# Stick-breaking attention scores: the low parts of two query tiles against the keys' high parts on the two row halves of TensorE, and projection units spread over all attention steps

## The chip, the cores and the metric

The kernel runs on one core of one Trainium2 chip. The metric is the device time of one execution in microseconds (us). A core has five engines: TensorE (PE; its weight loads are listed apart as PEld), VectorE (DVE), ScalarE (ACT), GpSimd (POOL) and SyncE (SP). Each works through its own queue in order; they wait for one another by semaphores. ACT and SP also issue the DMA transfers (ACTq, SPq in the rows).

## The reference

One layer of a hybrid mixer over 2048 tokens of width 1024: a modulated RMS norm, one wide projection, three kinds of mixing side by side (four heads of gated linear attention, GLA; four of HGRN, computed in the same chunked way; four of stick-breaking attention), a gated output projection and a last norm. The part that the change touches is the stick-breaking attention, with four heads of 64:

```python
def stick_breaking_attn(q, k, v):
    ...
    for i in range(t // SB_BLOCK):
        ...
        z = jnp.einsum('bhtd,bhsd->bhts', q_blk, k_blk).astype(jnp.float32) * scale
        ...
        log_beta = jax.nn.log_sigmoid(z)
        log_1m_beta = jnp.where(strict, jax.nn.log_sigmoid(-z), 0.0)
        between = lax.cumsum(log_1m_beta, axis=3, reverse=True) - log_1m_beta
        weights = jnp.where(strict, jnp.exp(log_beta + between), 0.0)
        outs.append(jnp.einsum('bhts,bhsv->bhtv', weights.astype(v.dtype), v_blk))
```

Everything is fp32 in the reference.

## The kernel before

The kernel runs in stages: modulation, norm and the first projections (to about 340 us), value columns and forget gates, the attention stage (402 to 870 us), the recurrent stage of GLA and HGRN (to about 1080 us), and the output projection.

**Split numbers.** A projection is done in a faster number format of TensorE (`F32R`), with each fp32 operand split into a high and a low part and three products: high by high, high by low and low by high. A *unit* (`fm_unit`, lines 149 to 157) is one such projection of 128 columns over 512 tokens: 24 matmuls of 128x512 (L154, L155, L156).

**Attention.** `sb_stream` (L680 on) yields 80 steps. Its loops run over the four heads, over the eight pairs `ip` of query tiles of 128 tokens (u = 0, 1 in a pair), and over the blocks `J` of 512 keys from the diagonal down. The query's tile `Q` holds the high part in `Q[:, 0]` and the low part in `Q[:, 1]`, each twice: on rows 0 to 63 and again on rows 64 to 127. The keys' tile `K[J]` holds the high part on rows 0 to 63 and the low part on rows 64 to 127. So L725 forms high times high plus high times low, and L726 adds low times high plus low times low, each with all 128 rows. A step does, for each u: two score matmuls into a PSUM tile `zt` (three buffers, `psZ`), a sigmoid on ACT (L728, tile `f`), on the diagonal a mask on POOL (L730), a running product on DVE along the keys (L734), up to four transpositions on PE (L738, tile `pt`), and a copy to `PT` on ACT for u = 0 (L741) or DVE for u = 1 (L743). Then come the products with the values (L750, tile `av`), whose 64 columns of output go to the lower half of the partitions for u = 0 and the upper half for u = 1. In the 32 steps whose block holds the diagonal a query tile has 1 to 4 of the 128-key sub-blocks, in the other 48 all four.

**Order.** In this stage a scheduler in the compiler sets the order on each engine from the order in which the program records the work. `interleave` (L760 on) records one step of `sb_stream` or one of 34 units of `fm_stream` (L668 on: the GLA and HGRN features and the gates), five units ahead of the first step and then in the proportion `na` to `nb`. Before, `na` is 80 // 2 = 40, so the units are used up when about half of the 80 steps are recorded. A unit is also held back until the last `av` matmul of two steps earlier has been issued (`SB_LAG`, `marks`). Further gate projections (L260) fill the recurrent stage that follows.

**Elsewhere.** In the output stage `normalise` spreads the eight norm factors over the partitions with L1157, a matmul with 40 rows, 128 columns of weights and 512 streamed columns, which stands among the full matmuls L1192 to L1194; L1137 and L1138 sum squares with 8 columns of weights. In the recurrent stage L917 forms small scores on row halves and column strips, L847 the state updates `U`.

Of the kernel before, what the change touches and what calls it, by code (L numbers as in the profile page):

```python
# [8 lines left out]
F32 = mybir.dt.float32  # L9
F32R = mybir.dt.float32r  # L10
# [8 lines left out]
P = 128  # L19
# [11 lines left out]
SB_LAG = 2  # L31
# [11 lines left out]
def hybrid_mixer_kernel(ctx, tc, x, c, w_ada, b_ada, w_in, w2, bg, gnw, lbl, hnw,  # L43
                        w_out, fnw, masks, sel2, out):
    nc = tc.nc
    mm = nc.tensor.matmul
# [4 lines left out]
    def dram(name, shape, dt=F32):  # L51
        return dp.tile(shape, dt, name=name)
# [6 lines left out]
    s_kc = [dram(f"s_kc{j}", [2, P, T]) for j in range(2)]  # L59
# [75 lines left out]
    def split_w(col0, pool, ncols, step, bufs=None, low=nc.vector):  # L135
        hi = pool.tile([P, KT, ncols], F32R, tag="whi", name="whi", bufs=bufs)
        lo = pool.tile([P, KT, ncols], F32R, tag="wlo", name="wlo", bufs=bufs)
        for s in range(0, ncols, step):
            raw = wp.tile([P, KT, step], F32, tag="wraw", name="wraw")
            nc.sync.dma_start(raw, w_in_v[:, :, col0 + s:col0 + s + step])  # L140
            nc.scalar.copy(hi[:, :, s:s + step], raw)
            low.tensor_tensor(lo[:, :, s:s + step], raw, hi[:, :, s:s + step].bitcast(F32),
                              op=ALU.subtract)
        return hi, lo
# [139 lines left out]
    with tc.manual_schedule(engines={ENG.PE, ENG.DVE, ENG.Activation, ENG.Pool}):  # L284
# [170 lines left out]
        for i in (1, 2):  # L455
            n = ORDER[i]
# [8 lines left out]
    n = ORDER[3]  # L465
# [173 lines left out]
    st2 = ExitStack()  # L639
    kp = st2.enter_context(tc.tile_pool(name="kp", bufs=5, reuse_waits="tile"))  # L640
# [27 lines left out]
    def fm_stream(blocks, after):  # L668
        for col0, chunks, evac in blocks:
            w = split_w(col0, wp, P, P)  # L670
            for n in chunks:
                mark = after()
                if mark is None:
                    fm_unit(w, n, evac)
                else:
                    with tc.issue_after(mark):
                        fm_unit(w, n, evac)
                yield

    def sb_stream(st):  # L680
        sp = st.enter_context(tc.tile_pool(name="sp", bufs=4, reuse_waits="tile"))
        vp = st.enter_context(tc.tile_pool(name="vp", bufs=5, reuse_waits="tile"))
        psZ = st.enter_context(tc.tile_pool(name="psZ", bufs=3, space=PSUM))
        psT = st.enter_context(tc.tile_pool(name="psT", bufs=2, space=PSUM))
        psO = st.enter_context(tc.tile_pool(name="psO", bufs=1, space=PSUM))
        NT = T // P
        for h in range(4):
            j, r0 = h // 2, (h % 2) * 64
            cs = slice(h * 64, (h + 1) * 64)
            vb, vp_ = (s_vc[e:T + e, cs].rearrange("(b p) d -> p b d", p=P) for e in (1, 0))  # L690
            V, Dd = [None] * 4, [None] * 4
            for J in reversed(range(4)):
                Js = slice(4 * J, 4 * J + 4)
                V[J] = vp.tile([P, 4, 64], F32, tag="V", name="V")
                Dd[J] = vp.tile([P, 4, 64], F32, tag="Dd", name="Dd")
                nc.sync.dma_start(V[J], vb[:, Js, :])
                nc.sync.dma_start(Dd[J], vp_[:, Js, :])
                nc.vector.scalar_tensor_tensor(Dd[J], V[J], nm, Dd[J], op0=ALU.mult, op1=ALU.add)
                nc.vector.scalar_tensor_tensor(V[J], V[J], nl, Dd[J], op0=ALU.mult, op1=ALU.add)
            K = [None] * 4  # L700
            for J in reversed(range(4)):
                K[J] = kp.tile([P, 512], F32R, tag="K", name="K")
                for r in range(2):
                    nc.sync.dma_start(K[J][r * 64:(r + 1) * 64].bitcast(F32),
                                      s_kc[j][r, r0:r0 + 64, J * 512:(J + 1) * 512])
            for ip in reversed(range(NT // 2)):
                Q = kp.tile([P, 2, 256], F32R, tag="Q", name="Q", bufs=2)
                for r in range(2):
                    nc.sync.dma_start(
                        Q[r * 64:(r + 1) * 64].bitcast(F32),  # L710
                        s_qc[j][:, r0:r0 + 64, ip * 256:(ip + 1) * 256].rearrange("l p t -> p l t"))
                av = psO.tile([P, P], F32, tag="av", name="av")
                carry = [1.0, 1.0]
                Jtop = (2 * ip) // 4
                for J in reversed(range(Jtop + 1)):
                    top = J == Jtop
                    PTs = []
                    for u in range(2):
                        i = 2 * ip + u
                        nb = (i % 4) + 1 if top else 4  # L720
                        n = nb * P
                        N = max(n, 256)
                        zt = psZ.tile([P, 512], F32, tag="zt", name="zt")
                        us = slice(u * P, (u + 1) * P)
                        mm(zt[:, 0:N], Q[:, 0, us], K[J][:, 0:N], start=True, stop=False)  # L725
                        mm(zt[:, 0:N], Q[:, 1, us], K[J][:, 0:N], start=False, stop=True)  # L726
                        f = sp.tile([P, 512], F32, tag="f", name="f")
                        nc.scalar.activation(f[:, 0:n], zt[:, 0:n], AF.Sigmoid, scale=-0.125)  # L728
                        if top:
                            nc.gpsimd.affine_select(f[:, n - P:n], f[:, n - P:n], pattern=[[-1, P]],  # L730
                                                    base=0, channel_multiplier=1,
                                                    compare_op=ALU.is_gt, fill=1.0)
                        fr = f[:, 0:n][:, ::-1]
                        nc.vector.tensor_tensor_scan(fr, fr, fr, carry[u], op0=ALU.mult, op1=ALU.bypass)  # L734
                        carry[u] = f[:, 0:1]
                        pt = psT.tile([P, 4, P], F32, tag="pt", name="pt")
                        for b in range(nb):
                            nc.tensor.transpose(pt[:, b, :], f[:, b * P:(b + 1) * P], ident)  # L738
                        PT = sp.tile([P, 4, P], F32, tag="PT", name="PT")
                        if u == 0:  # L740
                            nc.scalar.copy(PT[:, 0:nb, :], pt[:, 0:nb, :])  # L741
                        else:
                            nc.vector.tensor_copy(PT[:, 0:nb, :], pt[:, 0:nb, :])  # L743
                        PTs.append((nb, PT))

                    for b in reversed(range(4)):
                        for u, (nb, PT) in enumerate(PTs):
                            if b < nb:
                                diag = top and b == nb - 1
                                last[0] = mm(av[u * 64:(u + 1) * 64, :], (Dd if diag else V)[J][:, b, :],  # L750
                                             PT[:, b, :], start=diag, stop=(J == 0 and b == 0))
                    yield
                ost = sp.tile([P, P], F32, tag="ost", name="ost", bufs=2)
                nc.scalar.copy(ost, av)
                for u in range(2):
                    i = 2 * ip + u
                    nc.scalar.dma_start(s_o[6 + j][r0:r0 + 64, i * P:(i + 1) * P],
                                      ost[u * 64:(u + 1) * 64, :])

    def interleave(a, na, b, nb, first, marks, lead=0):  # L760
        ia = ib = 0
        da = db = False
        for _ in range(lead):
            next(b, None)
            ib += 1
        while not (da and db):
            if not da and (db or ia * nb <= ib * na):
                with tc.issue_after(first):
                    da = next(a, a) is a
                marks.append(last[0].ins)  # L770
                ia += 1
            elif not db:
                try:
                    next(b)
                except StopIteration:
                    db = True
                ib += 1
# [6 lines left out]
    def ev_silu(dst):  # L784
        def f(ps, n):
            sg = stg.tile([P, 512], F32, tag="st", name="sg")
            with tc.issue_after(sig.ins):
# [6 lines left out]
    feat_blocks = []  # L794
# [3 lines left out]
    feat_blocks += [(C_QB + j * P, ORDER, ev_silu(s_feat["qb"][j])) for j in range(2)]  # L798
    feat_blocks += [(gate_cols[j], ORDER[2:], ev_silu(s_gate[j])) for j in range(8)]
    marks = []  # L800
    interleave(sb_stream(st2), 80 // 2, fm_stream(feat_blocks, lambda: marks[-SB_LAG] if len(marks) >= SB_LAG else None),
               34, sig.ins, marks, 5)
    st2.close()
    hpools[ORDER[3]].close()
# [513 lines left out]
```

## Time and profile before

| | |
|---|---|
| median of 3 runs | 1297.59 us (1294.85 to 1298.18) |
| profiled execution, its own time | 1294.26 us |
| its span, first to last instruction | 1292.2 us |
| mean granted TensorE clock | 0.976 |
| PE busy | 1212.9 us (94%) |
| DVE busy | 742.1 us (57%) |
| ACT busy | 471.7 us (37%) |
| POOL busy | 162.9 us (13%) |
| attention stage, first score matmul to last `av` matmul | 402.3 to 869.8 us |

Busy time of PE counts each matmul from its start to its modelled end, and neighbours overlap; the distance from one start to the next is what a matmul costs when PE is full. Idle time of an engine that does not bound a stage costs nothing. The rows that matter stand in a section of their own below.

### The profile page before, as it was taken

To read this page: it belongs to the slowest core of one execution; us is meant where nothing else is said; L and a number is where in the kernel's file an instruction comes from. 1 tells how busy PE (TensorE), PEld (TensorE's weight loads), DVE (VectorE), ACT (ScalarE), POOL (GpSimd) and SP (SyncE) were. 2 spreads that over 40 slices of the span, in tenths; PEclk is the share of its full clock that TensorE was granted. 3 is DMA by queue.
4 is the path that set the end of the run, shared out by engine and by line. 5 is a ranking of instruction groups with operands and counts; after the bars stand their busy time and mean duration, and the time that the engine had idled before them with its cause. 6 is when DMAs were issued, how large, how long until landed. Compare 5 with 4: busy or idle time off the path is not lost.

```text
span 1292.2 us, 22081 instructions
## 1 busy us (share of the span) xinstructions
PE 1212.9 (94%) x8682; PEld 991.8 (77%) x8682; DVE 742.1 (57%) x1268; ACT 471.7 (37%) x860; POOL 162.9 (13%) x197
## 2 busy tenths in 40 slices
PE   7899999999999789999999999998978897999997
PEld 7777789899998667777777776766867774777775
DVE  4866325700009873535545488877776768765652
ACT  3376423421115342322333244543333434253621
POOL 3210000000003300000000001012432312010000
PEclk8999999999999989999999999998988997999999
DMA  9765442422133341322323323127877657464621
GB/s 265 240 232 180 147 126 91 143 82 86 46 99 112 126 106 54 92 72 86 100 68 86 109 73 92 34 62 238 264 222 208 195 174 241 133 224 132 203 82 51
DMA packets 177566, 173.73 MB, mean 134 GB/s; under 512 B 39625, under 2 KB 131882, under 8 KB 177454
## 3 DMA queue, kind: packets, MB, share of 16 engines
q1 hardware_dynamic: 144970, 128.70, 33.7%
q10 hardware_dynamic: 32484, 43.54, 9.7%
q8 instruction: 70, 1.15, 0.4%
q14 instruction: 42, 0.34, 0.1%
HBM read 113.47 MB, written 58.73 MB: 133 GB/s over the span
## 4 chain that ended last, share of the span: by engine, by line
PE 62%; DVE 13%; DMA 6%; issue 5%; ACT 2%; POOL 1%; SPq 0%; ACTq 0%; POOLq 0%; DVEq 0%
PE av L750 6%; PE acc L154 5%; PE acc L156 5%; PE acc L155 5%; PE acc L166 4%; PE acc L168 4%; PE acc L167 4%; PE pt L738 4%; PE acc L260 4%; PE y L1194 4%; PE y L1192 4%; PE y L1193 4%; DMA kt<-s_kb 2%; DVE W L858 2%; DVE f L734 2%
## 5 line engine op out<-in xcount | busy, mean ns | idle before, releaser
L734 DVE TENSOR_TENSOR_SCAN f<-f 128x512 f32<-128x512 f32 (+3 forms) x160 | 169.9, 1091 | 22.0 <-ACT f L728 11.9
L154 PE MATMUL acc<-hTh,whi 128*128 128x512 f32 x400 | 160.1, 402 | 9.9 <-ACT st L185 4.3
L156 PE MATMUL acc<-hTh,wlo 128*128 128x512 f32 x400 | 157.5, 394 | 0.0
L155 PE MATMUL acc<-hTl,whi 128*128 128x512 f32 x400 | 157.4, 394 | 0.0
L166 PE MATMUL acc<-whi,hTh 128*128 128x256 f32 (+1 forms) x512 | 146.2, 285 | 1.5 <-ACT stt L193 1.5
L168 PE MATMUL acc<-whi,hTl 128*128 128x256 f32 (+1 forms) x512 | 145.8, 285 | 0.0
L167 PE MATMUL acc<-wlo,hTh 128*128 128x256 f32 (+1 forms) x512 | 145.6, 284 | 0.0
L260 PE MATMUL acc<-hTh,whi 128*128 128x512 f32 x240 | 103.8, 432 | 1.7 <-ACT hTh L244 1.7
L260 PE MATMUL acc<-hTl,whi 128*128 128x512 f32 x240 | 97.9, 408 | 4.3 <-DVE hTl L250 4.3
L1192 PE MATMUL y<-wh,hTh 128*128 128x512 f32 x256 | 101.8, 398 | 0.0
L1193 PE MATMUL y<-wl,hTh 128*128 128x512 f32 x256 | 101.6, 397 | 0.0
L728 ACT ACTIVATE f<-zt 128x512 f32<-128x512 f32 (+3 forms) x160 | 82.1, 537 | 52.9 <-DVE f L734 24.7
L1194 PE MATMUL y<-wh,hTl 128*128 128x512 f32 x256 | 100.1, 395 | 0.4 <-DVE hTl L1160 0.4
L166 PEld LDWEIGHTS acc<-whi,hTh 128*128 128x128 f32 x512 | 97.8, 191 | 1.9 <-ACT stt L193 1.7
L154 PEld LDWEIGHTS acc<-hTh,whi 128*128 128x128 f32 x400 | 75.5, 189 | 29.9 <-ACT st L185 5.6
L167 PEld LDWEIGHTS acc<-wlo,hTh 128*128 128x128 f32 x512 | 97.8, 191 | 0.1
L168 PEld LDWEIGHTS acc<-whi,hTl 128*128 128x128 f32 x512 | 97.8, 191 | 0.1
L260 PE MATMUL acc<-hTh,wlo 128*128 128x512 f32 x240 | 97.4, 406 | 0.0
L750 PE MATMUL av<-PT,V 128*64 128x128 f32 x960 | 89.7, 282 | 0.6 <-DVE PT L743 0.6
L156 PEld LDWEIGHTS acc<-hTh,wlo 128*128 128x128 f32 x400 | 75.3, 188 | 17.0 <-issue 1.4
L738 PE MATMUL pt<-ident,f 128*128 128x128 f32 x544 | 87.0, 283 | 0.9 <-DVE f L734 0.7
L155 PEld LDWEIGHTS acc<-hTl,whi 128*128 128x128 f32 x400 | 75.6, 189 | 15.2 <-issue 1.0
(206 smaller groups left out, 2106.8 us busy)
## 6 DMA issues: line engine op xcount, KB each, us to landing
wraw<-in_w_in_dram SPq DMA_DIRECT2D x36, 512.0 KB, 4.9
xt<-in_x_dram SPq DMA_DIRECT2D x16, 512.0 KB, 5.2
wa<-in_w_ada_dram SPq DMA_DIRECT2D x16, 512.0 KB, 5.6
Q<-s_qc SPq DMA_DIRECT2D x64, 128.0 KB, 3.1
ot<-s_o SPq DMA_DIRECT2D x32, 256.0 KB, 3.4
gt<-s_gate SPq DMA_DIRECT2D x32, 256.0 KB, 4.2
r<-in_x_dram SPq DMA_DIRECT2D x16, 512.0 KB, 5.6
out_dram<-r SPq DMA_DIRECT2D x15, 512.0 KB, 2.7
```

The source lines that it names most:

```text
L154: mm(ps, hi[:, k, :], th[:, k, :], start=(k == 0), stop=False)
L155: mm(ps, hi[:, k, :], tl[:, k, :], start=False, stop=False)
L156: mm(ps, lo[:, k, :], th[:, k, :], start=False, stop=(k == KT - 1))
L166: mm(o, th[:, k, s], hi[:, k, 0:ncols], start=(k == 0), stop=False)
L167: mm(o, th[:, k, s], lo[:, k, 0:ncols], start=False, stop=False)
L168: mm(o, tl[:, k, s], hi[:, k, 0:ncols], start=False, stop=(k == KT - 1))
L260: mm(ps, a[:, k, :], b[:, k, :], start=(k == 0 and i == 0), stop=(k == KT - 1 and i == 2))
L734: nc.vector.tensor_tensor_scan(fr, fr, fr, carry[u], op0=ALU.mult, op1=ALU.bypass)
L750: last[0] = mm(av[u * 64:(u + 1) * 64, :], (Dd if diag else V)[J][:, b, :], PT[:, b, :], start=diag, stop=(J == 0 and b == 0))
L1192: mm(y, oh[:, k, us], wh, start=(k == 0), stop=False)
L1193: mm(y, oh[:, k, us], wl, start=False, stop=False)
L1194: mm(y, ol[:, k, us], wh, start=False, stop=(k == KT - 1))
```

## The change

The low part of each query tile is multiplied with the keys' high part alone, with 64 rows: for u = 0 on rows 0 to 63, where `K` has it, and for u = 1 on rows 64 to 127, where a new tile `K2` holds a second copy of it. Low times low is no longer formed. Both tiles' `zt` are taken at the start of a step, and the program records the two full matmuls first (now L725) and then the two half ones (now L730). K2 costs one more load per head and block, and 10 KB per partition; the DMA scratch is cut to make room. `interleave` gets `na` = 80.

```diff
-            K = [None] * 4
+
+            K, K2 = [None] * 4, [None] * 4
             for J in reversed(range(4)):
                 K[J] = kp.tile([P, 512], F32R, tag="K", name="K")
+                K2[J] = kp.tile([P, 512], F32R, tag="K2", name="K2")
                 for r in range(2):
                     nc.sync.dma_start(K[J][r * 64:(r + 1) * 64].bitcast(F32),
                                       s_kc[j][r, r0:r0 + 64, J * 512:(J + 1) * 512])
+                nc.sync.dma_start(K2[J][64:128].bitcast(F32), s_kc[j][0, r0:r0 + 64, J * 512:(J + 1) * 512])
...
                     PTs = []
+                    zts = [psZ.tile([P, 512], F32, tag="zt", name="zt") for _ in range(2)]
+                    nbs = [((2 * ip + u) % 4) + 1 if top else 4 for u in range(2)]
                     for u in range(2):
-                        i = 2 * ip + u
-                        nb = (i % 4) + 1 if top else 4
+                        N = max(nbs[u] * P, 256)
+                        mm(zts[u][:, 0:N], Q[:, 0, u * P:(u + 1) * P], K[J][:, 0:N], start=True, stop=False)
+
+                    for u in range(2):
+                        N = max(nbs[u] * P, 256)
+                        hs = slice(u * 64, (u + 1) * 64)
+                        mm(zts[u][:, 0:N], Q[hs, 1, u * P:(u + 1) * P], (K, K2)[u][J][hs, 0:N],
+                           start=False, stop=True)
+                    for u in range(2):
+                        nb, zt = nbs[u], zts[u]
                         n = nb * P
-                        N = max(n, 256)
-                        zt = psZ.tile([P, 512], F32, tag="zt", name="zt")
-                        us = slice(u * P, (u + 1) * P)
-                        mm(zt[:, 0:N], Q[:, 0, us], K[J][:, 0:N], start=True, stop=False)
-                        mm(zt[:, 0:N], Q[:, 1, us], K[J][:, 0:N], start=False, stop=True)
...
-    interleave(sb_stream(st2), 80 // 2, fm_stream(feat_blocks, lambda: marks[-SB_LAG] if len(marks) >= SB_LAG else None),
+    interleave(sb_stream(st2), 80, fm_stream(feat_blocks, lambda: marks[-SB_LAG] if len(marks) >= SB_LAG else None),
...
-    nc = _bacc.Bacc("TRN2", target_bir_lowering=False, num_devices=1)
+    nc = _bacc.Bacc("TRN2", target_bir_lowering=False, num_devices=1,
+                    dynamic_dma_scratch_size=1024)
```

What the scheduler makes of it on PE, in attention steps without a unit. In the rows, `zt` is written from `Q` and `K`; `K_` with a number is K2. Before, in the second half of the stage:

```order
L725 MATMUL zt<-K,Q 128x512
L726 MATMUL zt<-K,Q 128x512
L725 MATMUL zt<-K,Q 128x512
L726 MATMUL zt<-K,Q 128x512
L750 MATMUL av<-PT,V 64x128 x7
L738 MATMUL pt<-ident,f 128x128 x4
L750 MATMUL av<-PT,V 64x128
```

And with the change, where L746 is the transposition and L758 the product with the values:

```order
L725 MATMUL zt<-K,Q 128x512
L730 MATMUL zt<-K,Q 128x512
L725 MATMUL zt<-K,Q 128x512
L730 MATMUL zt<-K_4314,Q 128x512
L758 MATMUL av<-PT,V 64x128 x8
L746 MATMUL pt<-ident,f 128x128 x4
L725 MATMUL zt<-K,Q 128x512
L730 MATMUL zt<-K,Q 128x512
L746 MATMUL pt<-ident,f 128x128
```

The places are the same, and each former L726 has become an L730. Over the whole stage the two L730 of a step stand next to each other in 19 of the 80 steps; the other 122 stand singly. What follows the 141 blocks is an `av` matmul 56 times and an instruction that uses the whole array 85 times. The `av` matmuls form 120 blocks before and 123 with the change.

The end of the stage on PE, with the change:

```order
L156 MATMUL acc<-hTh_1018,wlo 128x512
L746 MATMUL pt<-ident,f 128x128 x3
L725 MATMUL zt<-K,Q 128x256 x2
L730 MATMUL zt<-K,Q 128x256
L730 MATMUL zt<-K_7329,Q 128x256
L260 MATMUL acc<-hTh_137,whi 128x512
L260 MATMUL acc<-hTh_137,wlo 128x512
```

The last unit (L156) stands just ahead of the last step's scores, where before it stood about half-way through the stage. On SP's queue the units' weight loads (`wraw`) stand among the Q loads up to the end, and the first loads of the recurrent stage come as two sets of `bc`, `qt` and `kt` and two further `qt`, and then `Vn` and `W`; before, it was one set, then `Vn` and `W`.

## Rows read from the trace of the kernel before

**Rows 1.** The page: busy time by engine, and the chain that ended last.
```profile
PE 1212.9 (94%) x8682; PEld 991.8 (77%) x8682; DVE 742.1 (57%) x1268; ACT 471.7 (37%) x860; POOL 162.9 (13%) x197
...
PE 62%; DVE 13%; DMA 6%; issue 5%; ACT 2%; POOL 1%; SPq 0%; ACTq 0%; POOLq 0%; DVEq 0%
```

**Rows 2.** Busy time (instructions) in stretches of the attention stage; last row: L154 alone.
```profile
core 0: us, PE busy (x) PEld busy (x) DVE busy (x) ACT busy (x) POOL busy (x), PEclk, DMA share, GB/s
402.00:480.00 78.00, 65.29 (x315) 50.65 (x315) 65.88 (x102) 33.00 (x58) 20.27 (x16) 0.93 0.40 125
480.00:760.00 280.00, 278.26 (x1679) 218.33 (x1675) 141.36 (x171) 86.87 (x174) 14.62 (x32) 1.00 0.29 84
760.00:869.80 109.80, 104.51 (x876) 77.05 (x874) 94.17 (x113) 54.64 (x120) 12.82 (x28) 1.00 0.21 59
...
760.00:869.80 109.80, 0.00 (x0) 0.00 (x0) 1.00 0.21 59
```

**Rows 3.** Waits of PE, 480 to 870 us: total us, times, longest.
```profile
PE av L750 <- DVE PT L743: 4.7, 10, 1.1
```

**Rows 4.** Timeline of PE, output stage: start us, us, line, operation, shapes.
```profile
1184.42 0.39 PE L1194 MATMUL y<-wh,hTl 128*128 128x512 f32 x1
...
1185.10 0.39 PE L1194 MATMUL y<-wh,hTl 128*128 128x512 f32 x1
1185.42 0.49 PE L1157 MATMUL acc<-rh,bsel 40*128 40x512 f32 x1
1185.84 0.50 PE L1192 MATMUL y<-wh,hTh 128*128 128x512 f32 x1
1186.18 0.39 PE L1193 MATMUL y<-wl,hTh 128*128 128x512 f32 x1
...
1187.27 0.40 PE L1192 MATMUL y<-wh,hTh 128*128 128x512 f32 x1
```

**Rows 5.** Timeline of PE: array parts used in turn, attention and recurrent stage.
```profile
773.92 1.09 PE L750 MATMUL av<-PT,V 128*64 128x128 f32 x14
774.94 1.09 PE L738 MATMUL pt<-ident,f 128*128 128x128 f32 x8
...
878.08 1.09 PE L917 MATMUL scp<-eP,bc 64*32 64x64 f32 x64
```

**Rows 6.** Timeline of PE: a score matmul of 384 columns and the next.
```profile
797.03 0.33 PE L726 MATMUL zt<-K,Q 128*128 128x384 f32 x1
797.20 0.40 PE L725 MATMUL zt<-K,Q 128*128 128x512 f32 x1
```

**Rows 7.** Timeline of PE: two L1157 next to each other.
```profile
1179.21 0.39 PE L1193 MATMUL y<-wl,hTh 128*128 128x512 f32 x1
1179.53 0.73 PE L1157 MATMUL acc<-rh,bsel 40*128 40x512 f32 x2
1180.19 0.49 PE L1194 MATMUL y<-wh,hTl 128*128 128x512 f32 x1
1180.52 0.39 PE L1192 MATMUL y<-wh,hTh 128*128 128x512 f32 x1
```

**Rows 8.** Timeline of PE: `av` matmuls inside a unit.
```profile
562.66 0.39 PE L154 MATMUL acc<-hTh,whi 128*128 128x512 f32 x1
562.98 1.09 PE L750 MATMUL av<-PT,V 128*64 128x128 f32 x14
563.99 0.50 PE L155 MATMUL acc<-hTl,whi 128*128 128x512 f32 x1
564.33 0.39 PE L156 MATMUL acc<-hTh,wlo 128*128 128x512 f32 x1
```

**Rows 9.** Timeline of PE: matmuls with 8 columns of weights among full ones.
```profile
1118.84 0.39 PE L1193 MATMUL y<-wl,hTh 128*128 128x512 f32 x1
1119.07 0.39 PE L1138 MATMUL acc<-sql,sel 128*8 128x512 f32 x1
1119.30 0.39 PE L1194 MATMUL y<-wh,hTl 128*128 128x512 f32 x1
```

**Rows 10.** Timeline of PE, the last steps: in brackets the idle time and its releaser.
```profile
864.55 1.09 PE L750 MATMUL av<-PT,V 128*64 128x128 f32 x14 [0.33 <-DVE PT L743]
...
867.11 0.44 PE L750 MATMUL av<-PT,Dd 128*64 128x128 f32 x4 [0.77 <-DVE PT L743]
...
869.14 0.44 PE L750 MATMUL av<-PT,Dd 128*64 128x128 f32 x4 [0.61 <-DVE PT L743]
```

**Rows 11.** The loads of K: ns to issue min/median/max, first and last start us; landing.
```profile
L704 SPq DMA_DIRECT2D K<-s_kc x32: 444/588/857, 354.6 to 792.4; - x32
...
DMA to landing us min/median/max: 2.8/3.4/3.9
```

**Rows 12.** Timeline of SP and PE: a W load of the recurrent stage and the first U.
```profile
873.92 0.58 SPq L824 DMA_DIRECT2D W<-s_va  x1
...
881.74 1.10 PE L847 MATMUL U<-Vn,KTt 64*64 64x128 f32 x32
```

## The prediction

> **What bounds the kernel now.** I read the page first: TensorE is busy 94% of the span, VectorE 57%, and the chain that ended last runs mostly through PE [rows 1]. Then the attention stage by itself, from its first score matmul at 402 us to its last `av` matmul at 869.8 us [rows 2]: PE is idle 12.7 us of the first 78, 1.7 us of the next 280 and 5.3 us of the last 110. VectorE is busy 301 of the 468 us; even in the last stretch, where no unit is left (L154 has no instruction there), it is at 94 of 110 us. So PE bounds the whole stage, with VectorE some 14% behind it in the last stretch, and a change here is worth what it does to PE's work. The few waits of PE behind VectorE's PT copy come to 4.7 us over 10 times [rows 3]. That is all the idle time that a better spread of the units could fill.
>
> The busy digits hide one thing, because a matmul's record is longer than its share of the engine. I therefore read starts, not durations. Full 128x512 matmuls in a row start 0.227 us apart: three of them go from 1184.42 to 1185.10 [rows 4].
>
> **What the change takes away.** A step had four score matmuls, each 512 columns. It still has four. Two are now full ones (high part of Q) and two use 64 rows each (low part of Q). The gain can only come if the two halves run at the same time. That parts of the array can do so is seen twice [rows 5]: 14 `av` records, which use two column halves in turn, take the 1.09 us of 8 transpositions of as many columns over the whole array, and in the recurrent stage 64 small score matmuls, on two row halves and two column strips of each, pass within 1.09 us, 17 ns each. But it needs the two halves to stand next to each other. In the scheduled order of the changed kernel (a piece of it stands above) that holds for 19 of the 80 pairs; the scheduler has put the second query tile's full matmul or other work between the others. Each of the 122 halves that stand alone still streams its 512 (or 384, 256) columns. Of the 19 pairs 7 are 512/512 and save 0.227 us each, 8 are 384/512 and save the shorter one, 0.17 us (L726 at 797.03, the next at 797.20 [rows 6]), and 4 are 256/256 and save about 0.12: 1.6 + 1.4 + 0.5 = **3.4 us**, or nothing if they do not run together. I take 3.4.
>
> **What it adds on PE.** The 160 half-array matmuls form 141 blocks (19 pairs, 122 single ones), each between instructions of another array shape. The trace has the same form of instruction elsewhere: L1157 in the output stage has 40 rows, so at most the array's lower half of rows, 128 columns of weights, 512 streamed columns and the same number type, between full matmuls. From the full one at 1185.10 over L1157 at 1185.42 and the full one at 1185.84 to the next at 1186.18 it takes 1.08 us for three matmuls [rows 4] that would take 0.68 without the change of shape: **0.40 us for one detour**. The next detour, 1186.18 to 1187.27, gives 1.09. Where two L1157 follow each other, the four go from 1179.21 to 1180.52, 1.31 us against 0.91 [rows 7]: again 0.40, so it is the two edges that are paid, not the half matmul. A detour to the 64-column `av` matmuls inside a unit shows the same two edges: 0.32 us in place of 0.23 before it (562.66 to 562.98) and 0.34 after it (563.99 to 564.33) [rows 8]. I take 0.20 us an edge.
>
> The nearest row that speaks against this is L1137 and L1138, which give only 8 columns of output: among full matmuls they start 0.23 us apart like any other [rows 9]. So a smaller matmul is not always charged, and the bounds of a detour are 0 and 0.40 us. I take 0.40, since L1157 agrees with the new instruction in rows, columns of weights and streamed columns, and L1137 in the last alone.
>
> After 85 of the 141 blocks a full-array instruction comes (a unit, a score matmul or a transposition): two new edges each, 85 x 0.40 = 34.0 us. After 56 an `av` matmul comes, whose entry was paid before as well: one new edge, 56 x 0.20 = 11.2 us. The `av` matmuls themselves now form 123 blocks instead of 120: 3 x 0.40 = 1.2 us. Together **46.4 us**, on the engine that bounds the stage. The mechanism is also worth more than the best that the change could give: even a neighbouring pair costs 0.40 of edges to save 0.23.
>
> The Trainium skill, page "TensorEngine Tiling (Array Packing)", section "Key Properties", says that changing the tiling mode, not just the tile, drains TensorE, and its section "Theoretical Speedup" promises up to a factor of two for contractions of at most 64. The first sentence has no price, and this trace shows one (rows 4, 7); the 8-column matmuls without a price (rows 9) agree with it only if they do not run in a mode of their own, which no row shows. The second sentence is the rival "as meant" below.
>
> **What it moves.** Units now run until the last steps instead of ending half-way. PE's idle of 1.7 us in the middle stretch and of 5.3 us in the last one could be filled, but 0.33 + 0.77 + 0.61 us of it stand after 864 us, in the last steps, where each product waits for its own chain [rows 10]; no unit is left there either. With PE slower, its waits behind VectorE shrink as well. I take **4 us** off; the bounds are 0 and 5.3. The 12.7 us of the first stretch stay: the order there is nearly the same.
>
> The 16 loads of K2 (128 KB each) go through SP's queue beside 32 equal ones for K, which take 0.59 us to issue and 3.4 us to land, the first one 48 us before the first score matmul [rows 11]. Nothing waits for K now; DMA is 29% busy there [rows 2]. I cost them at nothing; without that cover a head's first load would cost about 3.4 us, four times at most. The weights of the units (`wraw`) now stand between the Q loads on SP's queue and wait for VectorE; a Q load behind one can be late, 3 us each time. The recurrent stage's first V and W loads now stand behind two more `qt` loads that wait for VectorE; before, W was issued at 873.92 and its first user `U` ran at 881.74 [rows 12], so 0 to 3 us; I take 0, as gate units fill PE there. The smaller DMA scratch adds no instruction. SyncE, ScalarE (175 of 468 us) and GpSimd have room.
>
> **Sum.** The profiled execution took 1294.26 us, 3.3 below the median of 1297.59 us. 1294.3 - 3.4 + 46.4 - 4 = 1333.3; by the median it would be 1336.6. I forecast **1334 us**, 3% slower.
>
> **Rivals.**
> - *The half matmul is charged no edge* (chance 0.07). It would then be like L1137 [rows 9]. Left are the pairs, the idle time and the three `av` blocks: -3.4 - 4 + 1.2, about 1288 us, faster. Decisive is whether the full matmul before and after the half one keeps its 0.23 us. L1157 speaks against it in both of its patterns [rows 4, 7].
> - *Only one of the two costs at an edge remains* (0.09), for instance if the weights of the second shape load beside the first: 23 - 3.4 - 4 gives about 1310 us.
> - *As meant* (0.01): the queue brings all 80 pairs together, free of edges. 48 x 0.227 + 16 x 0.17 + 16 x 0.12 = 15.5 us saved, and 4 of idle time: 1275 us. The order speaks against it. By the skill's section "Theoretical Speedup" this is what should come.
> - *A new wait on top* (0.05): Q or first recurrent loads come late from SP's queue, 3 us each for some four of them: about 1345 us.
>
> **Numbers.** The forecast keeps a chance of 0.78, with a range of its own from 1323 (the 81 edges towards a transposition or an `av` matmul cost only the 0.09 us ahead of them, and all idle time is filled) to 1345 (no pair runs together, no idle time is filled, two loads are late). To hold 8 in 10 I reach to the half price and to part of the late loads: 1309 to 1346. A measurement of this kernel tells 0.3%, some 4 us, from nothing: faster 0.08, same 0.03 (between the free and the half-priced edge), slower 0.89.
>
> **What would show it.** In the changed profile a half-array matmul (L730) between full ones should start 0.32 us after the one ahead and hold PE 0.42 us; 19 pairs should start a few ns apart. The attention stage should last some 505 us instead of 468, with PE's idle time after the first 80 us no larger than now and VectorE's busy time unchanged. It would be wrong if L730 followed by a full matmul kept 0.23 us, or if PE's idle time grew by more than 5 us, which would mean that a load or VectorE has become the limit.

## The result, and the profile after

The changed kernel takes **1332.68 us** (median of 4 runs, 1328.59 to 1335.31) against 1297.60 us: a ratio of 1.0269 with a 95% interval of 1.0245 to 1.0293, slower by 35 us. The forecast was 1334 us.

The page of the changed kernel, busy time by engine and the chain that ended last (they answer to [rows 1]):

```profile
span 1333.3 us, 22085 instructions
...
PE 1256.4 (94%) x8682; PEld 994.9 (75%) x8682; DVE 738.1 (55%) x1268; ACT 472.8 (35%) x861; POOL 163.8 (12%) x197
...
PE 69%; DVE 9%; DMA 7%; ACT 2%; issue 2%; POOL 1%; SPq 1%; ACTq 0%; POOLq 0%; DVEq 0%
```

PE has as many instructions as before and is busy 43.5 us longer, while VectorE, ScalarE and GpSimd are within 4 us of where they were; PE's share of the chain went from 62% to 69%. The stretches of the attention stage in the changed kernel (window, length, then busy us with the number of instructions for PE, PEld, DVE, ACT, POOL; granted clock, DMA share, GB/s), to be laid beside [rows 2]:

```profile
402.00:480.00 78.00, 69.96 (x306) 51.19 (x304) 65.36 (x102) 32.26 (x58) 18.80 (x16) 0.91 0.41 127
480.00:760.00 280.00, 279.75 (x1702) 196.54 (x1701) 161.81 (x193) 94.92 (x196) 20.63 (x40) 1.00 0.27 77
760.00:903.70 143.70, 141.27 (x860) 100.94 (x859) 79.03 (x94) 51.19 (x104) 10.28 (x21) 1.00 0.26 75
```

The stage now ends at 903.7 instead of 869.8 us. PE is idle 8.0, 0.25 and 2.4 us in the three stretches; VectorE, at 94 of 110 us in the old last stretch, is at 79 of 144. How a half matmul passes is seen in the timeline of PE (start us, length us, line, operation, shapes):

```profile
624.43 0.48 PE L725 MATMUL zt<-K,Q 128*128 128x512 f32 x1
624.84 0.49 PE L730 MATMUL zt<-K,Q 64*128 64x512 f32 x1
625.26 0.44 PE L725 MATMUL zt<-K,Q 128*128 128x384 f32 x1
625.63 0.44 PE L730 MATMUL zt<-K,Q 64*128 64x384 f32 x1
626.00 0.66 PE L746 MATMUL pt<-ident,f 128*128 128x128 f32 x4
...
636.34 0.71 PE L725 MATMUL zt<-K,Q 128*128 128x512 f32 x2
636.98 0.50 PE L730 MATMUL zt<-K,Q 64*128 64x512 f32 x2
637.41 0.39 PE L725 MATMUL zt<-K,Q 128*128 128x256 f32 x1
```

A lone half of 512 columns holds PE from 624.84 to 625.26, 0.42 us, where a full matmul among its like holds it for 0.227. The full one behind it has 384 columns and, with a change of shape on both sides, takes 0.37 (625.26 to 625.63) in place of 0.17. At 636.98 both halves of a step stand together: the two also take 0.43 us. They do run at once, as meant, and a pair costs what a single one costs.

What becomes dear at a change of shape is seen on PEld, the weight loads. First a load inside a unit with its matmul, then the load of the lone half above, and then the loads of the pair at 636.98 and of the full matmul behind it:

```profile
628.55 0.19 PEld L156 LDWEIGHTS acc<-hTh,wlo 128*128 128x128 f32 x1
628.78 0.40 PE L156 MATMUL acc<-hTh,wlo 128*128 128x512 f32 x1
...
624.83 0.18 PEld L730 LDWEIGHTS zt<-K,Q 64*128 64x128 f32 x1 [0.24 <-issue]
...
636.98 0.18 PEld L730 LDWEIGHTS zt<-K,Q 64*128 64x128 f32 x2 [0.36 <-issue]
637.41 0.19 PEld L725 LDWEIGHTS zt<-K,Q 128*128 128x128 f32 x1 [0.25 <-issue]
```

Inside the unit the load starts 0.23 us ahead of its matmul and runs under the one before it. At a change of shape it starts together with its own matmul; over the stage that holds at all 471 changes (median 2 ns ahead, at most 31 ns, worked out from the trace). So a load is no longer hidden there. Its length alone is not the price: the loads of the `av` matmuls and the transpositions are shorter, 0.13 to 0.14 us, and yet their changes come to 0.20 us each (e5 below). Nor is it shape alone that holds a load back: behind a transposition, which uses the whole array, the load of a full matmul starts only 0.03 us ahead. What else is in the price of a change, no run separates.

### The profile page after: what moved, and what is told of

Read it like the earlier page. It is cut to its first block, busy times and chain, and to the rows that moved or that the text cites. A ratio compares the mean times of both kernels' runs of the same rounds, so it can differ in the third digit from the quotient of the medians.

```text
span 1333.3 us, 22085 instructions
## 1 busy us (share of the span) xinstructions
PE 1256.4 (94%) x8682; PEld 994.9 (75%) x8682; DVE 738.1 (55%) x1268; ACT 472.8 (35%) x861; POOL 163.8 (12%) x197
## 4 chain that ended last, share of the span: by engine, by line
PE 69%; DVE 9%; DMA 7%; ACT 2%; issue 2%; POOL 1%; SPq 1%; ACTq 0%; POOLq 0%; DVEq 0%
PE av L758 7%; PE acc L154 6%; PE acc L156 6%; PE pt L746 5%; PE acc L155 5%; PE acc L166 4%; PE acc L168 4%; PE acc L167 4%; PE y L1201 4%; PE y L1202 4%; PE y L1200 4%; PE zt L730 4%; PE acc L260 4%; PE zt L725 3%; DMA bc<-s_da 2%
## 5 line engine op out<-in xcount | busy, mean ns | idle before, releaser
L154 PE MATMUL acc<-hTh,whi 128*128 128x512 f32 x400 | 161.7, 405 | 8.4 <-ACT st L185 4.3
L156 PE MATMUL acc<-hTh,wlo 128*128 128x512 f32 x400 | 158.2, 396 | 0.0
L154 PEld LDWEIGHTS acc<-hTh,whi 128*128 128x128 f32 x400 | 75.4, 189 | 29.2 <-ACT st L185 5.4
L758 PE MATMUL av<-PT,V 128*64 128x128 f32 x960 | 91.3, 282 | 0.0
L751 DVE COPY PT<-pt 128x512 f32<-128x512 f32 (+1 forms) x80 | 50.4, 629 | 71.5 <-PE pt L746 71.2
L746 PE MATMUL pt<-ident,f 128*128 128x128 f32 x544 | 88.5, 286 | 0.7 <-ACT PT L749 0.4
L866 DVE SCALAR_TENSOR_TENSOR W<-W,SX,U 64x128 f32<-64x128 f32 (+1 forms) x248 | 77.8, 314 | 20.1 <-PE U L855 9.1
```

Of the source, the lines that this page charges most:

```text
L154: mm(ps, hi[:, k, :], th[:, k, :], start=(k == 0), stop=False)
L156: mm(ps, lo[:, k, :], th[:, k, :], start=False, stop=(k == KT - 1))
```

## The experiments

The theory: each change of the array's shape costs PE about 0.2 us, and the change adds 232 of them on the engine that bounds the stage. The rivals: the units' new places or the new loads cost the time (theory 2); or the halves are dear only when they stand alone. Shape changes were counted in the scheduled order of each kernel (the traces give the same numbers), from the first score matmul to the last `av` matmul. *PE work* is PE's busy time in that stretch, and *PE idle* what is left of it. A shape is the part of the array that a matmul uses: all of it, 64 rows (the halves) or 64 columns (the `av` matmuls). All are from one profile each; the times are medians, the ratios against runs of the kernel before on the same chip (not quotients of the medians, from which they differ by up to 0.2%). PE work repeats within 1 us from before to e0.

| kernel | shape changes | stage us | PE work us | PE idle us | time us | ratio (95%) |
|---|---|---|---|---|---|---|
| before | 239 | 467.0 | 447.3 | 19.7 | 1297.6 | |
| e0 before, again | 239 | 465.0 | 446.3 | 18.7 | 1300.3 (one run) | |
| changed | 471 | 500.6 | 489.9 | 10.7 | 1332.7 | 1.0269 (1.0245 to 1.0293) |
| e1 spread alone | 245 | 463.4 | 449.8 | 13.6 | 1297.9 | 1.0007 (0.9987 to 1.0027) |
| e2 full rows | 245 | 464.7 | 449.3 | 15.4 | 1300.4 | 1.0028 (1.0013 to 1.0043) |
| e4 all in pairs | 379 | 478.4 | 460.5 | 17.9 | 1313.8 | 1.0130 (1.0105 to 1.0155) |
| e8 one half | 383 | 486.3 | 474.4 | 11.9 | 1320.9 | 1.0175 (1.0154 to 1.0197) |
| e5 av together | 159 | 458.5 | 431.3 | 27.2 | 1291.2 | 0.9960 (0.9945 to 0.9976) |
| e6 the same, spread | 165 | 454.9 | 431.5 | 23.4 | 1288.7 | 0.9915 (0.9893 to 0.9938) |
| e7 av of two steps | 103 | 445.6 | 423.4 | 22.2 | 1280.4 | 0.9864 (0.9833 to 0.9895) |

e0, e8, e6 and e7 ran on a chip where the kernel before took 1300.2 us; e1, e2, e4 and e5 on one where it took 1297.7.

**e1, the spread alone.** The kernel before with

```diff
-    interleave(sb_stream(st2), 80 // 2, fm_stream(...
+    interleave(sb_stream(st2), 80, fm_stream(...
```

> The kernel before with the units spread over all 80 steps and nothing else: all score matmuls use the full array. Theory 1 (each change of the array's shape costs about 0.2 us on PE, and the half matmuls add 232 of them): there are 245 changes of shape instead of 239, so 1 us more, less 4 to 9 us of PE idle time that the units fill: 1289 to 1294 us. Theory 2 (the spreading itself, through SP's queue or late weights, costs the time): 1315 us or more.

Measured 1297.86 us: no difference that can be told, and above the 1289 to 1294 expected. Theory 2 falls for the spread. The stage is 3.6 us shorter than in the first profile of the kernel before and 1.6 us shorter than in its second (e0). A gain of 1.6 us lies inside the interval of the ratio, one of 2 us or more does not. The idle time filled, 5 to 6 us, is what was expected; but PE's work grew by 2.5 to 3.5 us where 1 was counted, and why is not shown.

**e2, full rows.** The changed kernel with the second score matmul over all rows again, so that low times low is formed again:

```diff
-                        mm(zts[u][:, 0:N], Q[hs, 1, u * P:(u + 1) * P], (K, K2)[u][J][hs, 0:N],
-                           start=False, stop=True)
+                        mm(zts[u][:, 0:N], Q[:, 1, u * P:(u + 1) * P], K[J][:, 0:N],
+                           start=False, stop=True)
```

> The changed kernel with the second score matmul back on all 128 rows of Q and K (low times low is formed again); the loads of K2, both score tiles taken at the step's start, and the spread stay. Theory 1: 245 changes of shape as in the run before, so within 3 us of it, about 1291 us. Theory 2 (loads, buffers, order): stays near 1333 us.

Measured 1300.42 us, 0.28% above the kernel before: within 3 us of e1, as expected, though not at 1291. The loads of K2, the two score tiles taken at once, the smaller DMA scratch and the spread are all in it, and together they cost some 4 us (interval 2 to 6). The other 32 us belong to the half matmuls, and the PE work differs by 40.6 us. The whole stage in the two kernels, full rows first:

```profile
401.90:866.60 464.70, 449.27 (x2858) 344.55 (x2857) 300.88 (x386) 177.35 (x357) 51.42 (x77) 0.99 0.30 87
```
```profile
403.10:903.70 500.60, 489.87 (x2859) 347.73 (x2857) 305.11 (x387) 178.37 (x357) 49.71 (x77) 0.99 0.29 84
```

PE works 40.6 us more on an equal number of instructions, of which 160 have fewer rows. DVE, ACT and POOL differ by less than 5 us.

**e4, all in pairs.** The changed kernel, with an order on PE that puts the two halves of a step behind one another:

```diff
-                        mm(zts[u][:, 0:N], Q[:, 0, u * P:(u + 1) * P], K[J][:, 0:N], start=True, stop=False)
+                        prev = mm(zts[u][:, 0:N], Q[:, 0, u * P:(u + 1) * P], K[J][:, 0:N], start=True, stop=False)
...
-                        mm(zts[u][:, 0:N], Q[hs, 1, u * P:(u + 1) * P], (K, K2)[u][J][hs, 0:N],
-                           start=False, stop=True)
+                        with tc.issue_after(prev.ins):
+                            prev = mm(zts[u][:, 0:N], Q[hs, 1, u * P:(u + 1) * P], (K, K2)[u][J][hs, 0:N],
+                                      start=False, stop=True)
```

> The changed kernel with an order edge that puts the two half matmuls of each step directly behind one another, so that all 80 pairs can run at once. Theory 1: 379 changes of shape instead of 471 and 80 pairs instead of 19. 80 blocks, 59 of them before full-array number-split matmuls at 0.40 us, 5 before transpositions at 0.35, 16 before av matmuls at 0.20: 28.5 us, less 15.5 us for the pairs, less about 9 us of idle time: 1298 us, perhaps some us more for score tiles that wait for a buffer. Rival (the halves cost nothing when paired, and only the lone ones are dear): 1294 - 15.5 - 9, about 1270 us.

Measured 1313.79 us. The rival (pairs are free: 1270) falls. Even with all 80 pairs running at once the kernel is slower than before. My number was 16 us too low. Of PE work I had counted 28.5 - 15.5 = 13 us above a kernel without halves; measured are 10.7 us against e1 and 11.2 against e2. So the price was right, and the 9 us of idle time that I took off did not come: PE is idle 17.9 us here, 2.5 us more than in e2; that the fixed order makes it wait is likely, but not shown. The rest is the base: I had started from 1294, a short execution (e0).

A piece of e4's timeline shows the pairs, two full matmuls, both halves, and the next thing:

```profile
706.68 0.71 PE L725 MATMUL zt<-K,Q 128*128 128x512 f32 x2
707.32 0.50 PE L731 MATMUL zt<-K,Q 64*128 64x512 f32 x2
707.75 0.38 PE L725 MATMUL zt<-K,Q 128*128 128x256 f32 x1
708.06 1.09 PE L759 MATMUL av<-PT,V 128*64 128x128 f32 x14
```

The two halves hold PE for 0.43 us (707.32 to 707.75), hardly less than the 0.45 us of two full ones, and the parts of the two edges that fall on their neighbours come on top: the full matmul of 256 columns behind the pair takes 0.31 us (to 708.06, where it has the edge to the `av` matmuls as well) instead of 0.12.

**e8, one half.** The changed kernel with u = 0 on all rows again (low times low is formed for that tile):

```diff
-                        mm(zts[u][:, 0:N], Q[hs, 1, u * P:(u + 1) * P], (K, K2)[u][J][hs, 0:N],
-                           start=False, stop=True)
+                        if u == 0:
+                            mm(zts[u][:, 0:N], Q[:, 1, 0:P], K[J][:, 0:N], start=False, stop=True)
+                        else:
+                            mm(zts[u][:, 0:N], Q[hs, 1, P:2 * P], K2[J][hs, 0:N], start=False, stop=True)
```

> The changed kernel with the half matmul for the second query tile alone; the first tile's second matmul is on all rows again, so no two halves can pair. 80 lone half matmuls, 383 changes of shape, nearly as in the run with 80 pairs (379). Theory 1 (edges by their count, and paired halves run at once): above the run with full rows (1300.4 us) by 53 x 0.40 + 5 x 0.35 + 22 x 0.20 = 27 us, less some us of idle time: 1322 to 1327 us, and above the run with 80 pairs (1313.8 us) by up to 15 us, the worth of the pairing. Rival (pairing gives nothing, a half matmul is cheap by itself): equal to the run with pairs or below it, 1310 to 1314 us.

Measured 1320.85 us, 1 us below the range of theory 1 and above the rival's; on this chip the kernel before is 2.5 us slower than on that of e2 and e4, so the distances to them by time are that much too large. It has nearly as many shape changes as e4 and no pair; PE works 13.9 us more than in e4, of the 15.5 us that 80 pairs should be worth. Against e2 there are 138 shape changes more and 25.1 us of PE work: 0.18 us each.

**e0, the kernel before once more.**

> The kernel before, unchanged, for a second profile: how far its stages vary from one execution to the next. The attention stage (467.0 us from first score matmul to last av matmul in the first profile) should repeat within 1 us; what comes after it took 413.0 us there and 417 to 422 us in the five other kernels, whose code there is the same. If it is 417 or more here, the difference after the stage is the variation of one execution; if it is 413 again, something in the changed order costs 4 us after the stage.

One execution of 1300.29 us. The stretch after the attention stage, in the first profile of the kernel before, then in this one, then in the changed kernel:

```profile
869.50:1292.20 422.70, 381.39 (x3324) 297.88 (x3321) 273.96 (x527) 150.86 (x254) 78.14 (x84) 0.95 0.59 182
```
```profile
868.90:1298.30 429.40, 381.18 (x3324) 297.68 (x3321) 273.37 (x527) 151.08 (x254) 77.39 (x84) 0.95 0.59 179
```
```profile
903.70:1333.30 429.60, 382.09 (x3324) 298.63 (x3321) 265.82 (x524) 148.29 (x250) 77.00 (x83) 0.94 0.59 177
```

The work is the same to 1 us, and the time is 6.7 us longer in the second execution of the same kernel. To the last matmul, as the expectation counted, it is 420 us, so its first case holds. In the eight profiles of other kernels here, on both chips, the stretch takes 427 to 432 us: it is the first profile of the kernel before, at 422.7, that is short. So the 7 us that the changed kernel seems to lose after the stage need no cause in the change; the medians, 35 us apart, leave some 1.5 us outside the stage. What makes this stretch longer or shorter was not tried, nor whether the chip has a part in it. The attention stage repeats within 2 us, not within the 1 us expected.

**e5, av together.** If shape changes are dear, having fewer of them must help without any half matmul. In the kernel before, the first product of a step uses u = 0, whose PT is ready early; it is issued alone, and the other seven follow after the transpositions of u = 1. One line of the kernel before makes the later tile go first:

```diff
-                        for u, (nb, PT) in enumerate(PTs):
+                        for u, (nb, PT) in reversed(list(enumerate(PTs))):
```

> The kernel before, with one line changed: the products with the values take u = 1 first, so that the first of a step waits for the later of the two PT copies and all of a step's av matmuls stand together: 80 blocks instead of 120, 159 changes of shape instead of 239. Theory 1: 80 changes fewer at 0.15 us (towards fp32 instructions) to 0.20 us: 12 to 16 us faster, 1282 to 1286 us, less of it where VectorE is nearly the bound (760 to 870 us): up to 1288. Rival (changes of shape are hidden behind other waits of PE): 1295 to 1300 us, or slower if PE waits for PT.

Measured 1291.23 us, faster by 0.4% (interval 0.24 to 0.55%); I had expected twice that, 1288 at the most. PE works 16.0 us less, 0.20 us for each of the 80 shape changes gone, just as the theory says. But 7.5 us came back as PE idle time. The first row of PE's waits from 480 to 861 us (line that waited, line waited for, total us, times, longest) shows where, against 4.7 us in [rows 3]:

```profile
PE av L750 <- DVE PT L743: 11.0, 18, 1.4
```

In a piece of its timeline the four score matmuls stand without a change of shape, 0.23 us apart but for the first behind the transpositions, and the last has the edge to the `av` matmuls, 0.33 us:

```profile
801.36 0.47 PE L725 MATMUL zt<-K,Q 128*128 128x512 f32 x1
801.67 0.39 PE L726 MATMUL zt<-K,Q 128*128 128x512 f32 x1
801.90 0.40 PE L725 MATMUL zt<-K,Q 128*128 128x512 f32 x1
802.13 0.40 PE L726 MATMUL zt<-K,Q 128*128 128x512 f32 x1
802.46 0.45 PE L750 MATMUL av<-PT,Dd 128*64 128x128 f32 x4
802.73 0.38 PE L750 MATMUL av<-PT,V 128*64 128x128 f32 x2
```

**e6, the same with the units spread** (e5's line and e1's).

> The kernel before with all of a step's av matmuls together and the units spread over all 80 steps. 165 changes of shape. Theory 1: the shape changes that fell with the av matmuls together were worth some 16 us of PE work, of which 7.5 us came back as PE waits in the part of the stage without units; with units everywhere these waits are filled: 74 to 80 changes fewer at 0.20 us, attention stage 449 to 453 us instead of 467, whole 1283 to 1287 us. Rival (the step's chain through VectorE sets the pace whatever stands on PE): no gain over 1291 us.

Measured 1288.70 us, 0.85% faster than before. Time and stage (454.9 us) lie above the 1283 to 1287 and 449 to 453 expected: the units fill the last stretch (PE idle 4.2 us after 760, against 10.2 in e5), but the middle one has 9.6 us of idle time, where e5 has 6.1.

**e7, av of two steps.** From e6, the products of two neighbouring steps of one query pair are issued together, the later step first; seven PT buffers, and the DMA scratch cut to 1024:

```diff
+                    held.append((J, top, PTs))
+                    if len(held) == 2 or J == 0:
+                        for J_, top_, PTs_ in reversed(held):
+                            for b in reversed(range(4)):
+                                for u, (nb, PT) in reversed(list(enumerate(PTs_))):
...
+                                        last[0] = mm(av[u * 64:(u + 1) * 64, :], (Dd if diag else V)[J_][:, b, :],
+                                                     PT[:, b, :], start=fresh[u], stop=left[u] == 0)
...
+                        held = []
```

> As the run before it, with the av matmuls of two steps held back and issued together (52 blocks, 103 changes of shape, seven PT buffers, DMA scratch of 1024). Theory 1: 62 changes fewer at 0.15 to 0.20 us, 9 to 12 us below the run with one block per step: 1272 to 1277 us, unless the later end of a pair of steps makes PE wait at the stage's end (2 to 3 us). Rival (the gain by fewer blocks is exhausted, waits take over): equal or slower.

Measured **1280.44 us**, 1.36% faster than the kernel before (interval 1.05 to 1.67%) and the fastest here. Against e6, 62 shape changes fewer took 8.1 us off PE's work, 0.13 us each, and 9.3 us off the stage. It misses its range by 3 us. This chip's runs lie about as much higher, but the price of a change is also below the 0.15 to 0.20 us expected, and why is not shown.

## Why the prediction was right

- **The price of an edge.** Taken from L1157 at 0.40 us a detour [rows 4, 7]: a half holds PE for 0.42 us and the next full one pays again. From the profiles of whole stages: changed kernel against e2, 40.6 us and the 3.4 us of 19 pairs, over 226 shape changes, is 0.195 us each; e8 against e2 0.18; e5 against before 0.20. The choice between 0 (L1137, L1138 in [rows 9]) and 0.40 by nearness of the form held; behind an 8-column matmul the load of the full one does run ahead (at 1119.07 for the matmul at 1119.30), so nothing there looks like a change of shape. The 0.32 us ahead of a half came too, where a unit's matmul stands there (429.31 to 429.62); behind a transposition or another half the full matmul has an edge or a slow start of its own, and it is 0.41 to 0.43.
- **The sum on PE.** Predicted 46.4 - 3.4 = 43.0 us. PE's work in the stage went from 447.3 to 489.9, 42.6 us. One part was a little high and hidden in this: e8's 25.1 us stand against 27 counted.
- **The pairs.** At once, at 0.43 us for both; 19 of 80 in number, as read in the order.
- **The idle time.** Taken at -4 us; it fell by 9.0, from 19.7 to 10.7. From 480 us on it fell by 4.3, as said; the step that failed is "the 12.7 us of the first stretch stay": they fell to 8.0. In e1, without halves, they are 9.0, so most of that comes with the spread. One wait before, of an `av` matmul for VectorE's PT copy, is 4.4 us of the 12.7; in e1 such waits come to 0.8 us and in the changed kernel to 1.4. The stage was therefore 500.6 us and not 505.
- **The moved loads.** Costed at nothing. In e2, which has them all, the time is some 4 us above before, with everything else that e2 changes; PE's waits from 480 us on name VectorE, ScalarE and no load in the changed kernel.
- **The base.** The sum was made on an execution that was short by some 6 us after the stage, which e0 showed later. On the median it would have been 1336.6, 4 us above the measured time, about the idle time that went beyond the estimate. That 1334 came within 2 us is luck in part: a base 3.3 us below the median and 5 us of idle time too few taken off nearly cancel.
- **Slips without weight.** The upper end of the forecast's own range, 1345, comes to 1347 by its terms (3.4 + 4 + 6 above 1333.3). VectorE's 14% in the last stretch is its idle share; against PE's 104.5 us of work it is 10% behind.
- **The rivals.** No price at an edge (1288) and half a price (1310) are refuted by the timeline, and the condition given for the second, weights that load beside the first shape, by the loads, which start with their own matmul; the queue brings only 19 pairs together, and e4, which brings 80, is still 1.3% slower than before, so "as meant" would not have come even then. The Trainium skill, page "TensorEngine Tiling (Array Packing)", section "Theoretical Speedup", gives up to twice the speed where a dimension is at most 64. The trace agrees for halves that stand together: the second is free, 0.43 us for two. The Trainium skill, same page, section "Key Properties", says that a change of tiling mode drains the engine. The trace shows what a change costs, 0.40 us for there and back, more than the 0.23 us gained, and not whether the engine empties.

## What to carry to other kernels

Two matmuls on halves of the array save at most one matmul's columns, so put against it the shape changes ahead of and behind the pair: here 0.40 us for a detour against 0.23 us for 512 columns, so a pair by itself is a loss: with all 80 together (e4) the kernel is still 1.3% slower. Several pairs in a row would share the two changes; by these numbers two would be just ahead (0.46 against 0.40), an estimate that no run here tests. Look for an instruction of the new form in the old trace and read starts, not lengths, around it: 24 instructions in another stage gave the price. The same price shows where a tuned kernel loses already: letting the products wait for the later tile and holding two steps together removed 136 of 239 shape changes and gave 1.36%, and of e5's 16 us of saved work half came back as idle time, and with the units spread (e6) still a quarter.

## What was not expected of the hardware

At a change of the array's shape no weight load of the stage ran ahead of its matmul: 2 ns at the median of the 471 changes, against 0.23 us inside a unit.

The stretch after the attention stage, with 381 us of PE work in both, took 422.7 us in one execution of the kernel before and 429.4 in another. A single profile can mislead by as much as half a per cent there, more than some of the effects studied here.
